# Laying column sums out over the partitions: two TensorE transposes or eight small DMAs

## The chip, the cores and the metric

The kernel runs on one core of a Trainium2 chip. The metric is the device time of one execution in microseconds; the figure that counts is the median of several runs. A profiled execution adds a trace of every instruction on the engines: TensorE (PE, with its weight loads as PEld), VectorE (DVE), ScalarE (ACT), GpSimd (POOL) and SyncE (SP), which in this kernel issues every DMA.

## What is computed

Two layers of a conditioned decoder trunk, for 256 positions of 1024 channels. Each layer is a feed-forward half-step, a token mixer (sparse attention beside a gated MLP), and another feed-forward half-step. Every one of these six sub-layers is entered through an RMS norm with a shift and a scale, and left through a gate, all three computed from one conditioning vector c:

```python
for l in range(DEPTH):
    mod = (jax.nn.silu(c) @ ada_w[l] + ada_b[l]).reshape(B, 3, 3, 1, D)
    n = _modulate(_rmsnorm(h, norm_g[l, 0]), mod[:, 0, 0], mod[:, 0, 1])   # xn * (1 + scale) + shift
    h = h + 0.5 * mod[:, 0, 2] * _swiglu(n, ffn_w_in[l, 0], ffn_w_out[l, 0])
    ...                                    # mixer: mod[:, 1, :], no factor 0.5
    n = _modulate(_rmsnorm(h, norm_g[l, 2]), mod[:, 2, 0], mod[:, 2, 1])
    h = h + 0.5 * mod[:, 2, 2] * _swiglu(n, ffn_w_in[l, 1], ffn_w_out[l, 1])
return _rmsnorm(h, final_g)
```

All is float32. The product of c with `ada_w` is what the change touches: 1024 x 1024 numbers for each of three vectors (m = 0 shift, m = 1 scale, m = 2 gate) of each of six sub-layers (si = 0 to 5).

## The kernel before, in words

The activations lie channel-major: `h` holds 128 partitions x 8 blocks x 256 positions, so channel 128k + p is partition p of block k. A vector over the channels must therefore lie as 128 partitions x 8 columns to be a per-partition scalar of an instruction.

**Weights.** `Stream` (L60 to L163) loads every weight block of 128 x 1024 float32 (`raw`, L116) from SP into one of 26 slots, in one fixed list. A block that goes to TensorE is split in two: `hi` by ScalarE (L134) and `lo` = raw − hi by VectorE (L135). A matmul of the reference becomes three, hi·hi, lo·hi and hi·lo. Blocks are loaded while at most 4 raw blocks (9 in some stretches) are unsplit, and split at most 6 or 7 blocks ahead of their use, so a slot becomes free when TensorE has used its block.

**The products with c.** The blocks of `ada_w` stand in the same list. They never go to TensorE: `ada_item` has VectorE multiply each by the 128 entries of silu(c) that belong to it and add it up in `acc` (128 x 1024, L252 for the first block and L255 for the seven others). What is left is a sum over the 128 partitions. `ada_step` does that in steps; it is called after each output block of a feed-forward sub-layer (L605, L670) and at places in the last product of the mixer (L1208, L1210). In one step, four matmuls with ones (L282) sum the columns of `acc`: quarter t of the 1024 sums lands, replicated, on partitions 32t to 32t + 31 of a PSUM bank, and ScalarE copies the 128 x 256 result into the SBUF tile `adas` (L286, one buffer). In the next step, two transposes on TensorE (L267) turn the sums so that they lie over the partitions; VectorE picks the 8 columns out of the PSUM bank and adds `ada_b` (L271) into the tile `md{si}_{m}`; for the scale it forms (1 + scale)·norm_g (L274), for the gate half of it (L276).

`ada_plan` (L350) says during which sub-layer which vectors are made: 16 of them in this way, four during sub-layer 0, two during 1, four during 2, five during 3, one during 5. All but the two during sub-layer 1 come well ahead of their use. Those two, shift and scale of the second feed-forward sub-layer, (2, 0) and (2, 1), are made inside the last product of the first mixer, by a hook that stands after parts of that product (L1210), some 10 us ahead of the entry that reads them.

**The entry.** `enter` (L418 to L518) begins each later sub-layer. For each of eight channel blocks VectorE adds the gated output of the previous sub-layer to `h` (L439), ScalarE multiplies it by the scale (L441, `uhi`, the hi part) and squares it (L442), and VectorE forms the lo part (L434, `ulo`). The shift enters as two extra columns (L429, L430). TensorE then starts the sub-layer's first product on these (L456) while the norm's factor is still being computed (L463, L400, L414), and the later products run on the normalized `nhi`, `nlo` (L487, L488, L491, L617). The output products of a feed-forward sub-layer and the mixer's last product are `acc_mm` (L563).

**Order.** TensorE, SP and GpSimd run in the order in which the program writes its instructions (`tc.manual_schedule`, L178). The order on VectorE and ScalarE is set by a scheduler at compile time, from its own estimate of when each operand is there, with priorities (`high_priority`) for some.

Of the kernel before, what the change touches and what calls it, by code (L numbers as in the profile page):

```python
# [18 lines left out]
F32 = mybir.dt.float32  # L19
# [147 lines left out]
def trunk(ctx, tc, xT, pk, cst, ada0, win7, ada, win, wou, mixw, mixv, w1, mp, wsT, lngb, bs, out):  # L167
    nc = tc.nc
    V, A, T, G = nc.vector, nc.scalar, nc.tensor, nc.gpsimd

    cp = ctx.enter_context(tc.tile_pool(name="cp", bufs=1))
# [15 lines left out]
    def bank(tag):  # L187
        return ps.tile([128, 512], F32, tag=tag, name=f"{tag}_{uid()}")

    def rbank():  # L190
        cnt["R"] += 1
        return bank(f"R{cnt['R'] % 4}")
# [31 lines left out]
    ident = cst_t[:, C_ID:C_ID + 128]  # L224
# [10 lines left out]
    def norm_g(si):  # L235
        return pk_t[:, 8 + si * 8:16 + si * 8]
# [3 lines left out]
    def ada_b(si):  # L240
        return pk_t[:, 64 + si * 24:88 + si * 24]
# [1 line left out]

    acc = {}
    mods = {}
    ready, summed, clock = [], [], [0]

    def ada_item(si, m, kb):
        def use(raw, slot):
# [10 lines left out]
    def ada_step(now=False):  # L260

        clock[0] += 1
        while summed:
            si, m, sm = summed.pop(0)
            p = rbank()
            for f in range(2):
                T.transpose(p[:, f * 128:(f + 1) * 128], sm[:, f * 128:(f + 1) * 128], ident)  # L267
            with tc.high_priority(PRIO_M):
                t = cp.tile([128, 8], F32, tag=f"md{si}_{m}", name=f"md{si}_{m}")
                v = p[:, 0:256].rearrange("p (f t r) -> p t f r", f=2, r=32)[:, :, :, 0]  # L270
                V.tensor_add(t.rearrange("p (t f) -> p t f", f=2), v,  # L271
                             ada_b(si)[:, m * 8:(m + 1) * 8].rearrange("p (t f) -> p t f", f=2))
                if m == 1:
                    V.scalar_tensor_tensor(t, t, 1.0, norm_g(si), op0=ALU.add, op1=ALU.mult)  # L274
                elif m == 2:
                    V.tensor_scalar(t, t, 0.5, None, op0=ALU.mult)  # L276
            mods[si, m] = t
        while ready and (now or clock[0] >= ready[0][2]):
            si, m, _ = ready.pop(0)
            p = rbank()  # L280
            for t in range(4):
                T.matmul(p[32 * t:32 * t + 32, 0:256], ones[:, 0:32], acc[si, m][:, t * 256:(t + 1) * 256],  # L282
                         start=True, stop=True, tile_position=(0, 32 * t))
            sm = tp.tile([128, 256], F32, tag="adas", name=f"adas{si}_{m}")
            with tc.high_priority(PRIO_M):
                A.activation(sm, p[:, 0:256], AF.Copy)  # L286
            summed.append((si, m, sm))
# [284 lines left out]
    def ffn(si, prev):  # L572
# [21 lines left out]
        if si == 0:  # L594
            with tc.manual_schedule(engines=START_ENGINES):
                x, zb = start()
            for j in range(4):
                evac(j, zb[j])
            accs = [bank(f"A{i}") for i in range(4)]
            for j in range(NS - 1):  # L600
                out_mm(j)
                if j + 4 < NS:
                    evac(j + 4, zb[j + 4])
                st.more()
                ada_step()  # L605
# [56 lines left out]
        for j in range(NS if si == 0 else 4, NF):  # L662
            r = in_mm(j)
            evac(j, r)
            st.more()
            for k in outs_after(si, j):
                out_mm(k)
                if k < NF - TAIL:
                    st.more()
                ada_step()  # L670
# [109 lines left out]
    def mix(si, l, prev):  # L780
# [423 lines left out]
        for kb in range(8 - WGROUP):  # L1204
            acc_mm(accs, [(st.next(), mhi[:, kb], mlo[:, kb])], kb == 0, False)
            st.more()
            if kb >= 2:
                ada_step()  # L1208
# [130 lines left out]
```

## Time and profile before

| quantity | us |
|---|---|
| median of three runs | 1156.9 |
| the three runs | 1155.82, 1156.9, 1160.89 |
| the profiled execution | 1160.77 |
| span of its trace | 1159.0 |
| PE busy | 1137.9 (98%) |
| DVE busy | 879.7 (76%) |
| ACT busy | 599.4 (52%) |

The span is the time from the first to the last instruction in the trace of the profiled execution. Busy time of an engine is the time during which at least one of its instructions ran. The granted TensorE clock is shown beside the trace as a share of full speed; over the span it was 0.987.

### The profile page before, as it was taken

To read this page: it belongs to the slowest core of one execution; us is meant where nothing else is said; L and a number is where in the kernel's file an instruction comes from. 1 tells how busy PE (TensorE), PEld (TensorE's weight loads), DVE (VectorE), ACT (ScalarE), POOL (GpSimd) and SP (SyncE) were. 2 spreads that over 40 slices of the span, in tenths; PEclk is the share of its full clock that TensorE was granted. 3 is DMA by queue.
4 is the path that set the end of the run, shared out by engine and by line. 5 is a ranking of instruction groups with operands and counts; after the bars stand their busy time and mean duration, and the time that the engine had idled before them with its cause. 6 is when DMAs were issued, how large, how long until landed. Compare 5 with 4: busy or idle time off the path is not lost. (4 is left out here: it accounts for less than half of the span.)

```text
span 1159.0 us, 23635 instructions
## 1 busy us (share of the span) xinstructions
PE 1137.9 (98%) x9630; PEld 1096.2 (95%) x9630; DVE 879.7 (76%) x1514; ACT 599.4 (52%) x1020; POOL 9.6 (1%) x13
## 2 busy tenths in 40 slices
PE   8999999989899999999999999999999999999998
PEld 6999999979799999999999999998899899999998
DVE  4998786778977799777579977767886778856543
ACT  3474444655575575444465444356656647544432
POOL 0000000000000000000000000000000000000000
PEclk8999999999999999999999999999999999999998
DMA  9979598438744659987647977974443366766600
GB/s 364 406 255 379 213 356 318 171 114 312 271 161 144 242 195 374 334 296 282 243 159 278 372 264 275 360 284 149 183 147 127 119 224 223 259 215 242 223 26 37
DMA packets 77180, 278.07 MB, mean 240 GB/s; under 512 B 8592, under 2 KB 9104, under 8 KB 77072
## 3 DMA queue, kind: packets, MB, share of 16 engines
q1 hardware_dynamic: 77072, 276.57, 65.1%
q8 instruction: 75, 1.23, 0.4%
q14 instruction: 33, 0.27, 0.1%
HBM read 275.49 MB, written 1.05 MB: 239 GB/s over the span
## 5 line engine op out<-in xcount | busy, mean ns | idle before, releaser
L135 DVE TENSOR_TENSOR lo<-raw,hi 128x1024 fp32r<-128x1024 f32 (+1 forms) x366 | 443.0, 1217 | 127.2 <-ACT hi L134 107.0
L134 ACT ACTIVATE hi<-raw 128x1024 fp32r<-128x1024 f32 (+1 forms) x366 | 381.0, 1052 | 273.3 <-PE R L617 67.0
L563 PE MATMUL A<-s1r,hi 128*128 128x256 f32 x1408 | 255.2, 279 | 0.0
L617 PE MATMUL R<-nhi,hi 128*128 128x256 f32 x1152 | 229.6, 281 | 0.0
L617 PE MATMUL R<-nhi,lo 128*128 128x256 f32 x1152 | 227.1, 279 | 0.0
L617 PE MATMUL R<-nlo,hi 128*128 128x256 f32 x1152 | 226.8, 279 | 0.0
L563 PEld LDWEIGHTS A<-s1r,hi 128*128 128x128 f32 x1408 | 218.9, 189 | 0.2 <-DVE s1r L555 0.2
L563 PE MATMUL A<-s1r,lo 128*128 128x256 f32 x704 | 196.0, 278 | 0.0
L617 PEld LDWEIGHTS R<-nhi,hi 128*128 128x128 f32 x1152 | 174.8, 188 | 5.8 <-issue 5.8
L617 PEld LDWEIGHTS R<-nlo,hi 128*128 128x128 f32 x1152 | 175.3, 189 | 0.0
L617 PEld LDWEIGHTS R<-nhi,lo 128*128 128x128 f32 x1152 | 175.0, 189 | 0.0
L255 DVE SCALAR_TENSOR_TENSOR acc<-raw,sc,acc 128x1024 f32<-128x1024 f32 x112 | 143.4, 1281 | 24.5 <-DMA raw<-in_ada 23.7
L563 PEld LDWEIGHTS A<-s1r,lo 128*128 128x128 f32 x704 | 132.3, 188 | 0.0
L583 ACT ACTIVATE s<-R 128x256 f32<-128x256 f32 x75 | 28.3, 377 | 105.1 <-PE R L617 105.1
L809 PE MATMUL A<-nhi,hi 128*128 128x256 f32 x256 | 74.8, 292 | 0.0
L809 PE MATMUL A<-nhi,lo 128*128 128x256 f32 x256 | 71.8, 280 | 0.0
L809 PE MATMUL A<-nlo,hi 128*128 128x256 f32 x256 | 71.8, 280 | 0.0
L554 ACT ACTIVATE s1r<-s 128x256 fp32r<-128x256 f32 x88 | 36.2, 412 | 47.9 <-DVE s L585 46.7
L585 DVE TENSOR_TENSOR s<-s,R 128x256 f32<-128x256 f32 x75 | 31.2, 416 | 37.1 <-ACT s L583 37.0
L809 PEld LDWEIGHTS A<-nhi,hi 128*128 128x128 f32 x256 | 49.0, 191 | 3.9 <-issue 2.3
L809 PEld LDWEIGHTS A<-nhi,lo 128*128 128x128 f32 x256 | 48.7, 190 | 0.0
L809 PEld LDWEIGHTS A<-nlo,hi 128*128 128x128 f32 x256 | 48.6, 190 | 0.0
(258 smaller groups left out, 1627.5 us busy)
## 6 DMA issues: line engine op xcount, KB each, us to landing
raw<-in_win SPq DMA_DIRECT2D x170, 512.0 KB, 5.7
raw<-in_ada SPq DMA_DIRECT2D x144, 512.0 KB, 5.7
raw<-in_mixw SPq DMA_DIRECT2D x92, 512.0 KB, 3.6
raw<-in_wou SPq DMA_DIRECT2D x88, 512.0 KB, 5.4
raw<-in_mixv SPq DMA_DIRECT2D x8, 536.0 KB, 5.7
w<-in_w SPq DMA_DIRECT2D x8, 512.0 KB, 8.5
raw<-in_win SPq DMA_DIRECT2D x8, 384.0 KB, 9.8
h<-in_xT SPq DMA_DIRECT2D x2, 512.0 KB, 5.5
```

Of the source, the lines that this page charges most:

```text
L134: self.nc.scalar.activation(hi[:, :n], raw[:, :n], AF.Copy)
L135: self.nc.vector.tensor_sub(lo[:, :n], raw[:, :n], hi[:, :n].bitcast(F32))
L255: V.scalar_tensor_tensor(a, raw[:, :D], sc[:, kb:kb + 1], a, op0=ALU.mult, op1=ALU.add)
L554: A.activation(hi_out, src, AF.Copy)
L563: T.matmul(accs[db // 2][:, (db % 2) * S:(db % 2 + 1) * S], w[:, db * 128:(db + 1) * 128], xx, start=(first and i == 0 and p == 0 and db % ...
L583: A.activation(s_, r[:, 0:S], AF.Silu)
L585: V.tensor_mul(g_, s_, r[:, S:2 * S])
L617: T.matmul(r[:, ab * S:(ab + 1) * S], W[:, c0:c0 + 128], xx[:, k], start=(i == 0 and ab == 0), stop=(i == 23), skip_group_check=True)
L809: T.matmul(r[:, b * S:(b + 1) * S], w[:, k], xx[:, k], start=(b == 0 and k == 0 and p == 0), stop=(k == 7 and p == 2), skip_group_check=True)
```

## The change

A vector goes from the sums to its place over the partitions by eight DMAs from SBUF to SBUF, one for each column of 128 channels, in place of the two transposes. Each reads 128 neighbouring numbers of one partition of `adas` and writes one number to each of the 128 partitions of `md`. They are issued from SP, at the step at which the transposes stood. The addition of `ada_b` no longer reads PSUM but `md` in place, and stands one step later, so a vector needs three steps in place of two. One PSUM bank of the ring `R` less is taken for each vector.

```diff
-    ready, summed, clock = [], [], [0]
+    ready, summed, turned, clock = [], [], [], [0]
...
-        while summed:
-            si, m, sm = summed.pop(0)
-            p = rbank()
-            for f in range(2):
-                T.transpose(p[:, f * 128:(f + 1) * 128], sm[:, f * 128:(f + 1) * 128], ident)
+        while turned:
+            si, m, t = turned.pop(0)
             with tc.high_priority(PRIO_M):
-                t = cp.tile([128, 8], F32, tag=f"md{si}_{m}", name=f"md{si}_{m}")
-                v = p[:, 0:256].rearrange("p (f t r) -> p t f r", f=2, r=32)[:, :, :, 0]
-                V.tensor_add(t.rearrange("p (t f) -> p t f", f=2), v,
-                             ada_b(si)[:, m * 8:(m + 1) * 8].rearrange("p (t f) -> p t f", f=2))
+                V.tensor_add(t, t, ada_b(si)[:, m * 8:(m + 1) * 8])
...
             mods[si, m] = t
+        while summed:
+            si, m, sm = summed.pop(0)
+            t = cp.tile([128, 8], F32, tag=f"md{si}_{m}", name=f"md{si}_{m}")
+            for k in range(8):
+                nc.sync.dma_start(t[:, k:k + 1], sm[k // 2 * 32:k // 2 * 32 + 1, k % 2 * 128:k % 2 * 128 + 128])
+            turned.append((si, m, t))
```

The lines of the changed kernel are L276 for the DMAs, L266 for the addition and L268, L270 for what follows it.

**TensorE at the first vector**, the gate of sub-layer 0, between an output product (L563) and the next input product (L617). In the kernel before:

```order
L563 MATMUL A_73_903<-s1r_1514,lo_1423 128x256
L563 MATMUL A_73_903<-s1r_1515,hi_1422 128x256
L267 MATMUL R_112_1665<-cst_t,adas_2_1565 128x128 x2
L617 MATMUL R_113_1671<-nhi_197,hi_1455 128x256 x2
L617 MATMUL R_113_1671<-nhi_197,lo_1456 128x256 x2
```

In the changed kernel:

```order
L563 MATMUL A_73_903<-s1r_1514,lo_1423 128x256
L563 MATMUL A_73_903<-s1r_1515,hi_1422 128x256
L617 MATMUL R_112_1674<-nhi_197,hi_1455 128x256 x2
L617 MATMUL R_112_1674<-nhi_197,lo_1456 128x256 x2
L617 MATMUL R_112_1674<-nlo_198,hi_1455 128x256 x2
```

The pair of transposes is gone and the input product takes the PSUM bank that they had; nothing else moves here.

**SP around the entry to the second feed-forward sub-layer**, whose shift and scale are `md_0_5063` and `md_1_5072` in the changed kernel. In the kernel before:

```order
L116 DMA raw_4985<-in_wou 128x1024
L116 DMA raw_5015<-in_win 128x1024
L116 DMA raw_5142<-in_win 128x1024
L116 DMA raw_5373<-in_wou 128x1024
L116 DMA raw_5379<-in_ada 128x1024
```

In the changed kernel:

```order
L116 DMA raw_5005<-in_wou 128x1024
L116 DMA raw_5035<-in_win 128x1024
L276 DMA md_0_5063<-adas_0_5042 128x1x1 x8
L276 DMA md_1_5072<-adas_1_5049 128x1x1 x8
L116 DMA raw_5172<-in_win 128x1024
L116 DMA raw_5403<-in_wou 128x1024
```

Both groups of eight DMAs stand one behind the other, and every later load behind them.

**ScalarE at the same entry**; `s` are squares, `hi` splits of weight blocks, `uhi` the entry's first operand. In the kernel before:

```order
L134 ACTIVATE hi_5138<-raw_4883 128x1024
L286 ACTIVATE adas_0_5022<-R_400_5017 128x256
L286 ACTIVATE adas_1_5029<-R_401_5024 128x256
L429 ACTIVATE uhi_5144<-md_0_5046 128x8x2
L441 ACTIVATE uhi_5144<-h,md_1_5051 128x256
L442 ACTIVATE s_404_5148<-h 128x256
```

In the changed kernel:

```order
L442 ACTIVATE s_403_5183<-h 128x256
L134 ACTIVATE hi_5399<-raw_4905 128x1024
L134 ACTIVATE hi_5405<-raw_4907 128x1024
L134 ACTIVATE hi_5468<-raw_4909 128x1024
L286 ACTIVATE adas_1_5049<-R_397_5044 128x256
L442 ACTIVATE s_404_5184<-h 128x256
L442 ACTIVATE s_405_5185<-h 128x256
L429 ACTIVATE uhi_5174<-md_0_5063 128x8x2
L199 ACT_TABLE_LOAD
L199 ACTIVATE junk_5225<-s_405_5185 128x1
L134 ACTIVATE hi_5474<-raw_4939 128x1024
L441 ACTIVATE uhi_5174<-h,md_1_5072 128x256 x8
```

The copy of the second vector's sums stood right behind that of the first; now six squares (the first five stand above the rows shown) and three splits stand between them, and all eight products with the scale come after the squares.

**VectorE at the same entry**, from the addition for the shift on. In the kernel before:

```order
L135 TENSOR_TENSOR lo_5139<-raw_4883,hi_5138 128x1024
L271 TENSOR_TENSOR md_0_5046<-R_402_5043,pk_t 128x8
L430 TENSOR_TENSOR ulo_5145<-md_0_5046,uhi_5144 128x8x2
L271 TENSOR_TENSOR md_1_5051<-R_403_5048,pk_t 128x8
L274 SCALAR_TENSOR_TENSOR md_1_5051<-md_1_5051,pk_t 128x8
L439 SCALAR_TENSOR_TENSOR h<-A_396_4877,md_2_2700,h 128x256 x2
```

In the changed kernel:

```order
L439 SCALAR_TENSOR_TENSOR h<-A_395_4900,md_2_2712,h 128x256 x2
L266 TENSOR_TENSOR md_0_5063<-md_0_5063,pk_t 128x8
L135 TENSOR_TENSOR lo_5406<-raw_4907,hi_5405 128x1024
...
L430 TENSOR_TENSOR ulo_5175<-md_0_5063,uhi_5174 128x8x2
L135 TENSOR_TENSOR lo_5469<-raw_4909,hi_5468 128x1024
L449 TENSOR_TENSOR s_398_5178<-s_398_5178,s_399_5179 128x256
L135 TENSOR_TENSOR lo_5475<-raw_4939,hi_5474 128x1024
L266 TENSOR_TENSOR md_1_5072<-md_1_5072,pk_t 128x8
L268 SCALAR_TENSOR_TENSOR md_1_5072<-md_1_5072,pk_t 128x8
L434 SCALAR_TENSOR_TENSOR ulo_5175<-h,md_1_5072,uhi_5174 128x256 x8
```

The two additions stood ahead of all the updates of `h` (L439); now they stand behind all of them, and the second behind three splits as well.

## Rows read from the trace of the kernel before

**Rows 1.** The page: span; busy time of the engines; the TensorE clock and the DMA share in 40 equal slices of the span (tenths); the chain that ended last, by engine.

```profile
span 1159.0 us, 23635 instructions
...
PE 1137.9 (98%) x9630; PEld 1096.2 (95%) x9630; DVE 879.7 (76%) x1514; ACT 599.4 (52%) x1020; POOL 9.6 (1%) x13
...
PEclk8999999999999999999999999999999999999998
DMA  9979598438744659987647977974443366766600
...
PE 28%; DVE 1%; DMA 0%; ACT 0%; issue 0%; ACTq 0%
```

**Rows 2.** The transposes and the addition behind them, each by source line: count, shortest/median/longest in ns, first and last start.

```profile
L267 PE MATMUL R<-cst_t,adas x32: 270/272/328, 126.0 to 1118.8; 128*128 128x128 f32 x32
...
L271 DVE TENSOR_TENSOR md<-R,pk_t x16: 155/164/168, 126.5 to 1119.1; 128x8 f32<-128x8 f32 x16
```

**Rows 3.** Timeline of PE at the first transposes: start in us, duration, instruction (x2: two in a row).

```profile
125.92 0.28 PE L563 MATMUL A<-s1r,hi 128*128 128x256 f32 x1
126.04 0.38 PE L267 MATMUL R<-cst_t,adas 128*128 128x128 f32 x2
126.17 0.48 PE L617 MATMUL R<-nhi,hi 128*128 128x256 f32 x2
126.49 0.40 PE L617 MATMUL R<-nhi,lo 128*128 128x256 f32 x2
```

**Rows 4.** PE alone in stretches between two places at which `ada_step` puts work on PE: window in us, its length, PE busy (instructions that touch the window), granted clock, DMA share, GB/s.

```profile
70.00:117.00 47.00, 47.00 (x417) 1.00 0.89 328
126.50:143.00 16.50, 16.50 (x143) 1.00 0.56 206
144.00:169.50 25.50, 25.50 (x217) 1.00 0.95 353
188.50:207.50 19.00, 19.00 (x163) 1.00 0.78 293
418.00:468.50 50.50, 50.50 (x448) 1.00 0.84 316
478.20:494.80 16.60, 16.60 (x143) 1.00 0.91 309
585.50:593.00 7.50, 7.50 (x66) 1.00 0.34 125
607.00:652.00 45.00, 45.00 (x383) 1.00 0.83 319
687.50:704.00 16.50, 16.50 (x142) 1.00 0.45 154
978.00:1109.00 131.00, 131.00 (x1159) 1.00 0.63 225
1119.20:1142.00 22.80, 22.80 (x196) 1.00 0.01 1
```

**Rows 5.** The entry to the second feed-forward sub-layer, timelines of PE, ACT and DVE (start in us, duration, instruction, and in brackets the idle time before it and what ended it).

```profile
393.94 0.38 PE L267 MATMUL R<-cst_t,adas 128*128 128x128 f32 x2
394.86 0.44 PE L267 MATMUL R<-cst_t,adas 128*128 128x128 f32 x2 [0.53 <-ACT adas L286]
...
404.67 0.40 PE L456 MATMUL R<-uhi,hi 128*128 128x258 f32 x2
...
417.11 0.40 PE L617 MATMUL A<-nhi,hi 128*128 128x256 f32 x2
...
394.42 0.38 ACT L286 ACTIVATE adas<-R 128x256 f32<-128x256 f32 x1 [1.49 <-PE R L267]
...
404.10 1.99 ACT L134 ACTIVATE hi<-raw 128x1024 fp32r<-128x1024 f32 x2
...
408.48 1.28 ACT L199 ACT_TABLE_LOAD   x1
...
404.87 0.88 DVE L439 SCALAR_TENSOR_TENSOR h<-A,md,h 128x256 f32<-128x256 f32 x2
...
408.64 2.36 DVE L135 TENSOR_TENSOR lo<-raw,hi 128x1024 fp32r<-128x1024 f32 x2
```

**Rows 6.** Issues on SP's queue: one load alone at its start and duration, and the page's groups of DMA issues (count, KB each, median us from issue to landing).

```profile
152.54 0.33 SPq L116 DMA_DIRECT2D raw<-in_win  x1
...
raw<-in_win SPq DMA_DIRECT2D x170, 512.0 KB, 5.7
raw<-in_mixw SPq DMA_DIRECT2D x92, 512.0 KB, 3.6
...
out_dram<-o SPq DMA_DIRECT2D x4, 256.0 KB, 2.1
...
pk_t<-in_pk SPq DMA_DIRECT2D x1, 104.0 KB, 2.0
```

**Rows 7.** All engines (PE, PEld, DVE, ACT, POOL busy and counts, then clock, DMA share, GB/s) behind a stretch in which PE idles, at 784.9.

```profile
784.90:788.30 3.40, 1.60 (x11) 1.19 (x11) 3.40 (x9) 3.40 (x9) 0.00 (x0) 1.00 0.56 206
788.30:791.70 3.40, 3.40 (x18) 3.40 (x18) 3.40 (x9) 1.75 (x3) 0.00 (x0) 0.50 0.01 2
```

**Rows 8.** ACT at the two places where a split waits for a load that stands behind a group's place on SP.

```profile
189.22 1.06 ACT L134 ACTIVATE hi<-raw 128x1024 fp32r<-128x1024 f32 x1 [0.73 <-DMA raw<-in_win]
...
758.87 2.27 ACT L134 ACTIVATE hi<-raw 128x1024 fp32r<-128x1024 f32 x2 [0.96 <-DMA raw<-in_win]
```

## The prediction

> **What bounds the kernel now.** The page first [rows 1]: PE is busy for 98% of the span at nearly full clock, and the chain that ended last lies on PE; DVE (76%) and ACT (52%) have slack, and the DMA share falls well below full in most slices. So the time is that of a row of matmuls, and an edit counts if it takes an instruction from that row, changes how far apart its matmuls stand, or makes PE wait. The transposes come next [rows 2]: 32, in 16 pairs. Their 0.27 us is a pipelined duration and no cost: the timeline at the first pair [rows 3] goes from one L563 over the pair and two L617 to the next L617 in 125.92 to 126.49 = 0.57 us. Three ordinary steps are 3 x 0.117 = 0.35, so a pair costs 0.22.
>
> Then the spacing of the matmuls [rows 4]. A window counts every matmul that touches it, about two more than fit. Less two, 70 to 117 gives 47.0 / 415 = 113.3 ns, 418 to 468.5 gives 113.2, 978 to 1109 gives 113.2. But 126.5 to 143 gives 117.0, 144 to 169.5 gives 118.6, 478.2 to 494.8 gives 117.7, 1119.2 to 1142 gives 117.5: at the same granted clock 1.00, PE goes at one of two paces. Contention doesn't explain it: the last stretch is slow with a DMA share of 0.01 and the one of 978 to 1109 is fast with 0.63. What the slow ones share is that a pair of transposes stands right ahead (125.9, 477.8, 1118.7); the fast ones follow the sums (L282) or a sub-layer without vectors. In all I count 17 slow stretches at or after a pair and before the next change of pace, 307 us; the rows show eight of them, the first and the last included. Lastly the entry to the second feed-forward sub-layer [rows 5], where vectors are made at the last moment: there PE goes from L563 to L456 (404.67) without a gap.
>
> **The pairs.** Fourteen pairs outside that entry x 0.22 = 3.1 us, all on the path: **−3.1**. The two at the entry are counted with it. DVE's addition (0.16 us, [rows 2]) only changes its operand.
>
> **The pace.** If all 307 us went at 113.2 in place of 117.6, that is 307 x 3.74% = 11.5 us. By sub-layer: 74 us in the first feed-forward, 2.8; 102 in the second, 3.8; in the third 52 that were slow from its entry on (585.5 to 593 and 607 to 652 have no pair between them) 2.0, and 56 behind further pairs, 2.1; 23 in the last, 0.9. The lower end is 0: the trace shows a pair ahead of the change of pace, not that nothing else would bring it, and the slow pace survived an entry. I take the first and last in full (3.7), since fast stretches stand on their other side, and just over half of the rest (4.2 of 7.9): **−7.9**.
>
> **The entry to the second feed-forward sub-layer.** In its rows [rows 5] both copies of the sums are done at 394.80, the additions follow the transposes at 394.86 at once, and the entry runs pair by pair behind L563. In the changed order the second copy stands on ACT behind six squares and three splits, and this is the one place where a vector has no spare step. Those splits follow the sixth square, which the third update of h releases; the two at 404.10 take 1.99, so three take 3.0. PE is done with L563 about 1 us earlier than now, as the wait of 0.53 and the two pairs are gone. I get three splits from about 401.7 to 404.7 and the copy (0.38) to 405. Then SP issues eight DMAs, each by the nearest row 0.33 us [rows 6], 2.7 us, to 407.7; the last lands 2.0 later by the two smallest transfers of the page (2.0 and 2.1; a load of 512 KB takes 3.6 to 5.7, the upper end), at 409.7. DVE's two short additions and ACT's first product with the scale (0.5) bring L456 to about **411.0**, against 404.67: +6.3, from +5.5 to +8.3. Ahead of these on DVE stand the last updates of h (404.87, 0.9) and three splits of 1.2 us [rows 5], which fit before 409.7, and on ACT a table load of 1.28. The L456 stretch now takes 404.67 to 417.11 = 12.4 us for 96 matmuls, 11.3 at the slow pace: it waits 1.1 for pairs of h, and those waits go, since h is long complete: −1.1. But PE idles some 7 us, and after an idle stretch the clock falls: behind one at 784.9 (busy 1.60 of 3.40) the next 3.40 us have 0.50 and 18 matmuls, 2.1 us of work at the full pace [rows 7], 1.3 lost. I take two such: +2.6. Entry: **+7.8**. Its lower bound is 0, if the scheduler's splits wait for nothing and the copy runs right after the sums; its upper bound 8.3 − 1.1 + 3 x 1.3 = 11.
>
> **SP's queue.** 128 DMAs of 0.33 us are 42 us of issue, off the path. But the last ones of a group wait in the compiled order for the landing of the load issued just ahead, so each group holds back the loads behind it for about 4 us [rows 6]. Splits run well ahead of PE nearly everywhere; at 189 and 759 they wait for a load [rows 8] behind a group's place and little cover is left. From 0 to 2 us each, taken near nothing since PE uses those blocks some 2 us after their split: **+0.5**. DVE's additions stand a step later, 8 us or more, behind the landing.
>
> **What the skill says against it.** Rows 2 and 3 price the transposes at 0.22 us a pair. The Trainium skill, VectorE: DVE Perf Modes, The three transpose paths, warns that a plain DMA copy which transposes by its access pattern is 19 times slower than the DMA's own transpose, 1309 ns for 128 x 128, and its Rules for kernel authors prefer TensorE. Eight of 128 rows by that would be 19 x 1309 / 16 = 1.6 us for a group (an estimate from that page), inside the 4.7 us reckoned above, and the sum stays; 1.6 us for each DMA one behind the other is the rival below. No row here shows such a DMA.
>
> **The sum** is −3.1 − 7.9 + 7.8 + 0.5 = **−2.7** against the profiled execution's 1160.8: 1158.1. That execution lies 3.9 above the median of 1156.9, so on the median's scale it is 1158.1 − 3.9 = 1154.2, rounded to **1154.0**; the rivals are given on that scale too.
>
> **The rivals.**
>
> *The pace returns in full.* For: the slow stretch at 1119 has nothing else near it but the pair. Against: 607 to 652. −3.1 − 11.5 + 7.8 + 0.5 = −6.3: 1150.6.
>
> *The entry is hidden.* The second copy finds its PSUM result and its place earlier than I think, and L456 starts where it does now. For: ACT is idle 1.49 us ahead of 394.42 [rows 5]. Against: the compiled order. −3.1 − 7.9 − 1.1 + 0.5 = −11.6: 1145.3.
>
> *The pace has another cause.* The sums or the loads set it, and only pairs are saved: −3.1 + 7.8 + 0.5 = +5.2: 1162.1, at the border of slower.
>
> *The small DMAs go one behind the other (slower).* A group then takes 8 x 2.0 = 16 us by the smallest transfers [rows 6], in place of 4.7. The entry waits 11.3 longer, and at 189 and 759 the loads behind each group come up to 9 later than cover allows: up to −2.7 + 11.3 + 18 = +27, 1183. It decides from about 3 us more per group on (three places, 8.5 in all). For: each writes 128 partitions one number at a time. Against: the larger loads overlap freely on the same queue. By the skill's 1.6 us each a group would take 12.4, and the time be about 1175.
>
> That the change doesn't do what it says is small here: the transposes are gone from PE's order.
>
> **How the numbers follow.** Forecast 0.42 (1154, its own range 1150 to 1160); full pace 0.24; entry hidden 0.08; other cause 0.13; one behind the other 0.13. A measurement of this kernel tells about 0.5% from no change: 1151.1 and 1162.7. Faster: 0.16 of the full pace, 0.08 and 0.11 of the forecast = 0.35. Slower: 0.13 and 0.05 of the other cause = 0.18. Same: 0.47. The range of 1145 to 1164 leaves out the DMAs one behind the other and a few hundredths on the low side.
>
> **What would show it.** L617 behind 126 at 113 ns in windows like those of rows 4 shows the pace right, 117 shows it wrong; the first L456 of that entry at 411 shows the entry, at 405 the hidden case; issue to landing of the L276 DMAs near 2 us against 10 tells the last rival; clock 0.50 in the stretch behind the entry shows the 2.6. It would be wrong above all if a pair were not what changes the pace, or if SP's queue held more than I see.

## The result, and the profile after

The changed kernel takes 1170.67 us (median of four runs, 1169.82 to 1175.22) against 1156.36 for the kernel before: a ratio of 1.0126, 95% interval 1.0086 to 1.0165, so slower by 14 us (1.3%) where 2 to 3 less were forecast. The profiled execution took 1175.22, 4.6 above its median, and the one of before lay 4.4 above its own (1156.36 is the median of four runs, the 1156.9 on record of three); the two spans, 1173.4 and 1159.0, differ by 14.4, and can be compared piece by piece.

The page of the changed kernel, against [rows 1]:

```profile
span 1173.4 us, 23793 instructions
...
PE 1133.9 (97%) x9598; PEld 1090.9 (93%) x9598; DVE 879.5 (75%) x1514; ACT 600.3 (51%) x1020; POOL 9.7 (1%) x13
...
PEclk8999998999999989999999999989999999999998
...
PE 28%; DVE 1%; DMA 0%; ACT 0%; issue 0%; ACTq 0%
```

PE is busy for 4 us less, though the span is 14 longer: PE waits. The clock row has three new dips, in slices 7, 15 and 27, at about 190, 425 and 780 us; each follows a stretch in which PE idled. The chain's shares look as before: a chain that runs along PE doesn't show waits of 10 us in 1170.

Where it happens is seen by setting the same instruction side by side, the first L456 of each of the five entries, from the two PE timelines, and the length of what lies between:

| PE at | before | after | later by | so this stretch |
|---|---|---|---|---|
| entry 1 (first mixer) | 216.6 | 220.0 | 3.4 | +3.4 |
| entry 2 (second feed-forward) | 404.7 | 417.7 | 13.0 | +9.6 |
| entry 3 (third) | 593.7 | 604.4 | 10.7 | −2.3 |
| entry 4 (second mixer) | 785.0 | 803.7 | 18.7 | +8.0 |
| entry 5 (last) | 964.0 | 981.1 | 17.1 | −1.7 |
| end of the span | 1159.0 | 1173.4 | 14.4 | −2.7 |

There are three losses and, where nothing waits, gains. The first loss is in the last input products ahead of the first mixer; PE, then ACT:

```profile
194.41 0.71 PE L617 MATMUL R<-nhi,hi 128*128 128x256 f32 x2 [3.40 <-ACT hi L134]
195.68 0.79 PE L617 MATMUL R<-nhi,lo 128*128 128x256 f32 x2 [0.55 <-DVE lo L135]
196.27 0.63 PE L617 MATMUL R<-nlo,hi 128*128 128x256 f32 x2
```

```profile
193.31 1.06 ACT L134 ACTIVATE hi<-raw 128x1024 fp32r<-128x1024 f32 x1 [0.97 <-DMA raw<-in_win]
194.57 1.06 ACT L134 ACTIVATE hi<-raw 128x1024 fp32r<-128x1024 f32 x1 [0.21 <-DMA raw<-in_win]
```

PE waits for a split, ACT for a load. Behind the waits the matmuls go in pairs of 0.63 instead of about 0.40, and the granted clock is 0.50, the lower of its two levels (1.2 of 2.4 GHz):

```profile
194.80:198.20 3.40, 2.85 (x14) 2.55 (x14) 3.23 (x3) 2.94 (x3) 0.00 (x0) 0.50 0.57 172
```

The instruction at 188.8 still ran 2.8 us ahead of its time in the kernel before, the one at 201.8 runs 4.3 behind: 7.1 lost. The same picture stands at 774 to 785, from 11.5 behind to 19.0, 7.5 lost; PE there:

```profile
778.15 0.77 PE L617 MATMUL R<-nhi,hi 128*128 128x256 f32 x2 [3.52 <-ACT hi L134]
```

The queue that should have brought the first of those loads:

```profile
151.66 6.14 SPq L276 DMA_DIRECT2D md<-adas  x8
157.91 0.53 SPq L116 DMA_DIRECT2D raw<-in_ada  x1
...
184.82 3.25 SPq L116 DMA_DIRECT2D raw<-in_win  x4
```

The four `in_win` loads for which ACT waits at 193 were issued at 180.41 in the kernel before, now at 184.82. And windows of the DMA share (window, length, PE busy, clock, DMA share, GB/s) show what became of the time, in the changed kernel, then two of them in the kernel before:

```profile
153.00:156.00 3.00, 3.00 (x29) 1.00 0.89 321
156.00:159.00 3.00, 3.00 (x29) 1.00 0.12 6
159.00:162.00 3.00, 3.00 (x29) 1.00 0.94 315
171.00:174.00 3.00, 3.00 (x29) 1.00 0.72 243
```

```profile
156.00:159.00 3.00, 3.00 (x28) 1.00 1.02 414
171.00:174.00 3.00, 3.00 (x29) 1.00 0.93 362
```

While the group holds SP for 6.1 us, what was queued ahead of it lands, and the DMA engines run dry: 0.12 at 156 to 159. In the kernel before they are near full throughout [rows 4: 0.95 from 144 to 169.5], so what isn't moved in the pause has little room later. At 171 the share falls once more: SP issued nothing from 165.33 to 170.95, a wait that the trace puts down to a split (DVE, `lo`) and that the kernel before doesn't have at this size; it follows the pause, though no run shows that it comes of it.

The third loss is the entry of which the prediction knew; SP, ACT, DVE and PE there:

```profile
397.27 17.90 SPq L276 DMA_DIRECT2D md<-adas  x16
...
409.81 0.36 ACT L286 ACTIVATE adas<-R 128x256 f32<-128x256 f32 x1
...
417.13 3.30 ACT L441 ACTIVATE uhi<-h,md 128x256 fp32r<-128x256 f32 x8 [3.78 <-DVE md L268]
...
416.73 0.17 DVE L266 TENSOR_TENSOR md<-md,pk_t 128x8 f32<-128x8 f32 x1 [2.10 <-DMA md<-adas]
```

```profile
417.69 0.80 PE L456 MATMUL R<-uhi,hi 128*128 128x258 f32 x2 [9.76 <-ACT uhi L441]
```

The chain of the forecast stands there link by link: second copy, eight issues, landing, addition, product, PE after 9.8 us of idling. The small DMAs by themselves:

```profile
L276 SPq DMA_DIRECT2D md<-adas x128: 469/599/1607, 118.2 to 1133.2; - x128
...
DMA to landing us min/median/max: 1.9/2.8/7.5
```

And the pace, in windows that answer to [rows 4], in the first, second, third and last feed-forward sub-layer:

```profile
119.00:142.00 23.00, 23.00 (x205) 1.00 0.55 190
512.00:543.00 31.00, 31.00 (x276) 1.00 0.86 321
619.00:663.00 44.00, 44.00 (x375) 1.00 0.84 323
1129.00:1163.00 34.00, 34.00 (x303) 1.00 0.02 2
```

Less the two that touch the edges, 203, 274, 373 and 301 matmuls: 113.3, 113.1, 118.0 and 113.0 ns. Fast where the kernel before was slow in three of them; the third is slow in both, and in the changed kernel it stays slow behind its sums too:

```profile
717.00:741.00 24.00, 24.00 (x206) 1.00 0.83 299
```

(204 matmuls, 117.6 ns.) So there no pair of transposes is needed for the slow pace.

### The profile page after: what moved, and what is told of

Its sections match the earlier page's. It is cut to its first block, busy times and chain, and to the rows that moved or that the text cites. A ratio compares the mean times of both kernels' runs of the same rounds, so it can differ in the third digit from the quotient of the medians.

```text
span 1173.4 us, 23793 instructions
## 1 busy us (share of the span) xinstructions
PE 1133.9 (97%) x9598; PEld 1090.9 (93%) x9598; DVE 879.5 (75%) x1514; ACT 600.3 (51%) x1020; POOL 9.7 (1%) x13
## 5 line engine op out<-in xcount | busy, mean ns | idle before, releaser
L563 PE MATMUL A<-s1r,hi 128*128 128x256 f32 x1408 | 252.0, 277 | 0.0
L617 PE MATMUL R<-nhi,hi 128*128 128x256 f32 x1152 | 229.5, 281 | 6.9 <-ACT hi L134 6.9
L617 PE MATMUL R<-nhi,lo 128*128 128x256 f32 x1152 | 228.1, 280 | 1.0 <-DVE lo L135 1.0
L617 PE MATMUL R<-nlo,hi 128*128 128x256 f32 x1152 | 227.5, 279 | 0.0
L563 PEld LDWEIGHTS A<-s1r,hi 128*128 128x128 f32 x1408 | 217.5, 188 | 0.2 <-DVE s1r L555 0.2
L563 PE MATMUL A<-s1r,lo 128*128 128x256 f32 x704 | 195.0, 277 | 0.0
L617 PEld LDWEIGHTS R<-nhi,hi 128*128 128x128 f32 x1152 | 176.0, 190 | 13.1 <-ACT hi L134 7.3
L617 PEld LDWEIGHTS R<-nhi,lo 128*128 128x128 f32 x1152 | 176.5, 191 | 1.6 <-DVE lo L135 1.6
L617 PEld LDWEIGHTS R<-nlo,hi 128*128 128x128 f32 x1152 | 176.7, 190 | 0.0
L563 PEld LDWEIGHTS A<-s1r,lo 128*128 128x128 f32 x704 | 132.1, 188 | 0.0
```

The source lines that it names most:

```text
L563: T.matmul(accs[db // 2][:, (db % 2) * S:(db % 2 + 1) * S], w[:, db * 128:(db + 1) * 128], xx, start=(first and i == 0 and p == 0 and db % ...
L617: T.matmul(r[:, ab * S:(ab + 1) * S], W[:, c0:c0 + 128], xx[:, k], start=(i == 0 and ab == 0), stop=(i == 23), skip_group_check=True)
```

## The experiments

All were compared with the kernel before. A table of what they gave; "idle" is PE's time beyond 0.113 us a matmul, summed over the steps above 0.15 us in the PE timeline, so waits and matmuls at half clock together, in the 33 us ahead of entry 1, at entry 2 and in the 33 us ahead of entry 4:

| kernel | us | ratio, 95% interval | idle at 194, entry 2, 776 |
|---|---|---|---|
| before | 1156.4 | | 0.6, 0.1, 0.6 |
| after | 1170.7 | 1.0126 [1.0086, 1.0165] | 7.4, 10.0, 7.5 |
| no layout | 1141.0 | 0.9859 [0.9831, 0.9887] | 0.5, 0.1, 0.9 |
| both | 1171.7 | 1.0125 [1.0095, 1.0155] | 6.9, 9 (inside L563), 6.8 |
| hybrid | 1161.4 | 1.0056 [1.0026, 1.0086] | 7.0, 0.1, 7.5 |
| direct | 1178.6 | 1.0182 [1.0150, 1.0213] | 0.1, 0.1, 0.1 |
| shift | 1148.2 | 0.9934 [0.9912, 0.9956] | 0.9, 0.1, 0.6 |
| GpSimd's queue | 1163.3 | 1.0076 [1.0047, 1.0104] | 5.2, 8.9, 3.5 |
| one DMA | 1148.5 | 0.9925 [0.9898, 0.9953] | 0.7, 3.0, 0.5 |
| VectorE | 1146.1 | 0.9920 [0.9889, 0.9951] | 0.8, 0.1, 0.5 |
| before again | 1159.1 | one run | 0.6, 0.1, 0.6 |
| shift by 64 | 1152.5 | 0.9961 [0.9946, 0.9977] | 0.6, 0.1, 0.6 |
| ring of buffers | 1171.2 | 1.0120 [1.0097, 1.0142] | 5.6, 7.8, 8.2 |
| one group | 1161.4 | 1.0043 [1.0023, 1.0063] | 4.2, 0.1, 0.6 |

**No layout (e1).** Neither the transposes nor the DMAs.

```diff
-            p = rbank()
-            for f in range(2):
-                T.transpose(p[:, f * 128:(f + 1) * 128], sm[:, f * 128:(f + 1) * 128], ident)
...
-                V.tensor_add(t.rearrange("p (t f) -> p t f", f=2), v,
-                             ada_b(si)[:, m * 8:(m + 1) * 8].rearrange("p (t f) -> p t f", f=2))
+                V.tensor_add(t, sm[:, 0:8], ada_b(si)[:, m * 8:(m + 1) * 8])
```

> Neither transposes nor DMAs: the addition takes the first 8 columns of the copied sums as they lie (so shift, scale and gate hold wrong numbers), all else as in the kernel before, the order at the entry to the second feed-forward sub-layer too. Theory A (a pair of transposes on TensorE costs its own 0.22 us and leaves the matmuls behind it 117.6 instead of 113.2 ns apart): 11 to 13 us below the kernel before, about 1144. Rival (the pace has another cause, the pairs cost only themselves): 3 to 4 us below, about 1153.

Measured 15.1 less. The matmuls go at 113 ns from the first vector to the last, in the third feed-forward sub-layer as well (a stretch of 44 us that is slow in both the others):

```profile
156.00:159.00 3.00, 3.00 (x29) 1.00 1.02 365
...
119.00:142.00 23.00, 23.00 (x205) 1.00 0.55 197
597.00:639.00 42.00, 42.00 (x372) 1.00 0.83 321
```

(203 in 23.0 and 370 in 42.0 us: 113.3 and 113.5.) So the pace and the pairs together are worth what the prediction put on them, and more, above the 11 to 13 that were expected. It didn't show yet that the pairs make the pace. The first row is the DMA share where the changed kernel has 0.12.

**Both (e2).** The kernel before with its transposes, and the eight DMAs besides.

```diff
             mods[si, m] = t
+            u = cp.tile([128, 8], F32, tag="mdx", name=f"mdx{si}_{m}")
+            for k in range(8):
+                nc.sync.dma_start(u[:, k:k + 1], sm[k // 2 * 32:k // 2 * 32 + 1, k % 2 * 128:k % 2 * 128 + 128])
```

> The kernel before with its transposes, and the eight DMAs of each vector besides, into a tile that nobody reads. Theory B (the groups of DMAs hold SP's queue for 5 to 8 us where the loads are near their limit, and TensorE pays for it at the last input products of the first and fourth sub-layer, 7 us each): 1171 to 1177, stalls at 194 and 776 as in the changed kernel, the pace of before, and some 5 us at the entry to the second feed-forward sub-layer since the second copy of sums waits for the DMAs to have read the first. Rival (the stalls come from the later addition or from another order on ScalarE and VectorE, not from the queue): within 3 us of before, 1154 to 1160.

Measured 15.5 more, with both stalls at nearly their size: the pairs being gone has no part in them, the DMAs make them. At the entry the second pair of transposes waits 8.92 us for the second copy, in the middle of L563:

```profile
396.67 0.38 PE L267 MATMUL R<-cst_t,adas 128*128 128x128 f32 x2
405.97 0.69 PE L267 MATMUL R<-cst_t,adas 128*128 128x128 f32 x2 [8.92 <-ACT adas L289]
```

One thing was not as expected. The pace behind the pairs:

```profile
125.00:141.00 16.00, 16.00 (x143) 1.00 0.65 237
150.50:166.50 16.00, 16.00 (x143) 1.00 0.80 294
518.00:542.00 24.00, 24.00 (x214) 1.00 0.83 311
```

141, 141 and 212 matmuls less the edges: 113.5, 113.5, 113.2. The pairs are all there and the pace behind them is fast. A pair can't be what sets it.

**Hybrid (e3).** The DMAs, but transposes for the two vectors of the second feed-forward sub-layer.

```diff
             si, m, sm = summed.pop(0)
+            if si == 2 and m < 2:
+                p = rbank()
+                for f in range(2):
+                    T.transpose(p[:, f * 128:(f + 1) * 128], sm[:, f * 128:(f + 1) * 128], ident)
...
+                continue
```

> The changed kernel with the transposes put back for the two vectors of the second feed-forward sub-layer alone. Theory B (that entry costs 11 us because the second copy, the eight issues and the landing stand in front of it): 1159 to 1161, L456 right behind L563 again, and the two 7 us stalls stay. Rival (the entry is late because the loads behind are late too): gains 5 us or less, 1165 or more.

Measured 1161.4, at the edge of what theory B gave; its ten runs lie from 1157.5 to 1170.0. The entry's wait is gone, which is worth 8 to 9 us against the changed kernel, the two stalls stay, and so does a loss against the kernel before.

**Direct (e4).** The sums made over the partitions by eight matmuls with the accumulated product as weights.

```diff
+            for k in range(8):
+                T.matmul(p[:, k:k + 1], acc[si, m][:, k * 128:(k + 1) * 128], ones[:, 0:1],
+                         start=(k == 0), stop=(k == 7), skip_group_check=True)
```

> Neither transposes, nor DMAs, nor the copy: the sums are made over the partitions at once, by eight matmuls with 128 columns of the accumulated product as weights and one column of ones as the moving operand; the addition follows in the same step. Theory A, if only the transposes change the pace: 10 to 13 us below the kernel before, 1143 to 1147, with the entry to the second feed-forward sub-layer a little earlier. If any float32 weight load of 128 x 128 changes the pace: about 1154 to 1157.

A miss on both sides, 22 us more. The timeline at the first vector:

```profile
118.73 1.84 PE L282 MATMUL R<-ones,acc 128*128 128x1 f32 x16
120.43 0.48 PE L621 MATMUL R<-nhi,hi 128*128 128x256 f32 x2
```

Eight matmuls stand as sixteen in the trace and take 1.7 us before the next product starts, in place of 0.22 for the pair and some 0.7 for the four sums, and the pace behind them is slow nearly everywhere. No stall: there are no small DMAs.

**Shift (e5).** The kernel before, with one more tile that nobody reads.

```diff
             mods[si, m] = t
+            u = cp.tile([128, 8], F32, tag="mdx", name=f"mdx{si}_{m}")
+            V.memset(u, 0.0)
```

> The kernel before with one more tile of 128 x 8 numbers, set to zero and read by nobody, so that all SBUF tiles behind it lie 32 bytes per partition further on, as they do in the kernel with transposes and unread DMAs; no DMA is added and TensorE's instructions are the same. Theory C (where the tiles lie, or something else that stays the same through a run, decides at which of two paces TensorE goes on behind a pair; the pair itself does not): 113.4 ns behind the pairs, 1144 to 1148. Rival (the pace behind a pair depends on how the DMAs or the waits move the moment of its start): 117.8 as before, 1154 to 1159.

Measured 1148.2, 7 to 8 us less, by a tile without use. Behind the pairs:

```profile
126.50:142.50 16.00, 16.00 (x138) 1.00 0.56 202
152.50:168.00 15.50, 15.50 (x139) 1.00 0.95 358
501.50:525.00 23.50, 23.50 (x210) 1.00 0.92 310
```

117.6 behind the first, then 113.1 and 113.0 where the kernel before has 117 to 118. Theory C holds for all but the first pair and the stretch behind entry 3. By the traces the order of instructions on PE, ACT and DVE is that of the kernel before, but for 16 zeroings of about 0.07 us on DVE, all done by 3.5 us from the start.

**GpSimd's queue (e6).** `nc.sync.dma_start` for the small DMAs becomes `nc.gpsimd.dma_start`.

> The changed kernel with its small DMAs issued from GpSimd's queue in place of SP's. Theory B (the loss is that SP's queue stands still, not what the small DMAs take of the DMA engines): no 7 us stalls at 194 and 776, the entry to the second feed-forward sub-layer still late by 5 to 11, 1148 to 1157. Rival (element by element writes take the DMA engines from the loads): the stalls stay, 1165 or more.

Between the two: 1163.3. The first stall falls from 7.4 to 5.2, the second from 7.5 to 3.5, and what is left has another cause. The loads come in time now: the split that waits for the first of them starts at 187.57, where it stood at 189.22 in the kernel before [rows 8] and at 193.31 in the changed one, and the DMA share at 156 to 159 is 0.71. But the small DMAs land later from here:

```profile
DMA to landing us min/median/max: 1.9/5.0/6.4
```

and on VectorE the addition, which waits until they have landed, stands ahead of a split; that split is late, and PE waits for it (DVE, then PE):

```profile
193.17 0.17 DVE L266 TENSOR_TENSOR md<-md,pk_t 128x8 f32<-128x8 f32 x1 [3.28 <-DMA md<-adas]
```

```profile
194.74 0.50 PE L617 MATMUL R<-nhi,lo 128*128 128x256 f32 x2 [1.78 <-DVE lo L135]
```

At 768.58 VectorE waits 4.36 in the same way, and PE 1.45 for its split. Waits of 0.76 behind a load's split are left at either place. So most of what SP's queue costs is gone in this run, and most of the rest is the addition's place ahead of the splits, with the lower clock behind each wait. The entry is hardly shorter (8.9).

**One DMA (e7).** `for k in range(8)` becomes `for k in range(1)`, with the tile zeroed at the start.

> The changed kernel with the first of the eight DMAs of each vector alone; the other seven columns are zero before ada_b is added, so shift, scale and gate are wrong there. Theory B: a group is one issue of some 0.5 us behind one wait, the stalls shrink to under 1 us each and the entry to 3 to 6 us: 1146 to 1152. Rival (what costs is that any DMA stands in the queue behind a wait for the copied sums): 1160 or more.

1148.5: no stalls, and the entry at 3.0 us. That any DMA stands there is not what costs; the length of the group is. A single one holds SP for about half a microsecond:

```profile
L277 SPq DMA_DIRECT2D md<-adas x16: 470/476/1122, 116.0 to 1102.1; - x16
```

**VectorE (e8).** The four sums read the product in another order of columns, and a mask picks.

```diff
+            av = acc[si, m].rearrange("p (c q i) -> p q c i", q=4, i=32)
             for t in range(4):
-                T.matmul(p[32 * t:32 * t + 32, 0:256], ones[:, 0:32], acc[si, m][:, t * 256:(t + 1) * 256],
+                T.matmul(p[32 * t:32 * t + 32, 0:256], ones[:, 0:32], av[:, t],
...
+                V.tensor_mul(smv, p[:, 0:256].rearrange("p (c i) -> p c i", i=32), m32[0][:, None, :].to_broadcast([128, 8, 32]))
+                V.tensor_reduce(t, smv, axis=AX, op=ALU.add)
+                V.tensor_add(t, t, ada_b(si)[:, m * 8:(m + 1) * 8])
```

> Neither transposes nor DMAs nor the copy: the sums read the accumulated product in another order of columns (blocks of 32 channels), so that each group of 32 partitions holds the channels that belong to it, and VectorE takes the right one of each 32 by a product with a mask and a sum over 32 columns; the addition follows, all in one step. The matmuls on TensorE are the four of the kernel before with a strided moving operand. Theory A or C: the pace stays at 113.4 ns and nothing waits: 1139 to 1144. If the strided operand is read slower or the four sums leave the slow pace: 1150 or more.

1146.1, 2 above the range, and the fastest of those that compute the whole trunk: 10 us below the kernel before, 25 below the changed one, with no stall. One stretch behind entry 3 is slow in it.

**Before again (e9)** and **shift by 64 (e10)**: the kernel before, unchanged, and the unread tile with 16 columns.

> The kernel before, unchanged, for a second trace. Theory C (the pace behind each pair is fixed by what the program is, not by chance of an execution): 117.8 ns behind the same pairs as in the first trace (7 of 8 that come from the fast pace), 113.4 behind the others, and about 1156. Rival (chance): another pattern.

> As the unread tile of 32 bytes per partition, but with 64. If the place of the tiles decides the pace: again another pattern behind the pairs than in the kernel before, of 1144 to 1158 according to it, and the pattern alone explains the time at 0.6 us lost for each 16 us at the slow pace. If the first unread tile was chance: 1156 with the pattern of the kernel before.

The second trace of the kernel before has the same pattern, pair for pair, the odd one out included (fast behind 661.5 in the first, behind 662.2 in the second):

```profile
126.50:143.00 16.50, 16.50 (x145) 1.00 0.58 207
505.70:530.70 25.00, 25.00 (x217) 1.00 0.91 311
...
663.00:679.00 16.00, 16.00 (x145) 1.00 0.96 347
```

(By start times of neighbouring matmuls behind the pairs 117.8, 117.8 and 113.3 ns; the windows end among the sums, whose matmuls count too.) With 64 bytes the pattern is a third one, and the time, 1152.5, lies between. So the pace behind a pair was the same in both executions of a program, and it differs between programs with the same instructions on TensorE. What differed is where the tiles lie, and the short zeroings at the start, more than 100 us ahead of the first pair; that it is the place of the tiles is the likelier of the two, and not shown apart.

**Ring of buffers (e11).** The copied sums go to a ring of eight (`sm = s1()`).

> The changed kernel, but the copied sums go to a ring of eight buffers of that size in place of one buffer; now the second copy stands right behind the first on ScalarE at the entry to the second feed-forward sub-layer. Theory D (the single buffer, read by DMAs, sends the second copy behind the squares and splits, and that is half of the entry's loss): that entry loses 3 to 6 us in place of 12.3, both 7 us stalls stay, 1162 to 1166. Rival (the entry's loss is the queue's alone): 1169 to 1172.

A miss: 1171.2, as the changed kernel. The copy does stand some 12 us further ahead, the 16 DMAs are issued by 407.3, but PE idles for 7.8 at the entry in place of 10.0: DVE takes the addition at 411.55, behind its splits, without a wait for a DMA. The buffer was 2 us of that entry, not half of it, and a gain of that size can't be told in the time.

**One group (e12).** The kernel before, with the DMAs for the vector (1, 0) alone: `if (si, m) != (1, 0):` stands around the transposes.

> The kernel before, with the eight DMAs in place of the transposes for one vector alone, (1, 0), whose group stands on SP some 40 us ahead of the stall at 194. Theory B as the traces now have it (a group empties the DMA engines for some 3 us while they are near full from there to the end of the sub-layer, so what is lost there is missing at 194): a stall of 3 to 6 us at 194 with half clock behind it, none at 776, and 0 to 3 us from another pace either way: 1157 to 1163. Rival (the group that stands right at 191 is what stalls TensorE): no stall, 1153 to 1157.

1161.4, and 4.2 us at 194, the half clock included, with none at 776 and nothing at the entry:

```profile
152.47 6.73 SPq L291 DMA_DIRECT2D md<-adas  x8
```

```profile
195.63 0.50 PE L632 MATMUL R<-nhi,hi 128*128 128x256 f32 x2 [2.32 <-ACT hi L134]
```

A group of 6.7 us at 152 makes PE wait at 193. It is the early group that is paid for at 194, not the one that stands beside it. What is left of the changed kernel's 7.4 would be the other three groups' of that sub-layer, which no run takes singly.

## Why the prediction was wrong

**The step that failed is "SP's queue": +0.5, measured 7.1 + 7.5 = 14.6.** Two things in it were wrong. The price: an issue of a small DMA was put at 0.33 by the row of a large one and took 0.60, and with the waits a group held the queue for 5.0 to 7.8 us in place of about 4. And above all the cover. The prediction asked at each place whether the next blocks were split early enough, and found thin cover at two places. But the blocks' lead is a stock that the loads fill, and the loads had the DMA engines near full from 144 on [rows 4]. A pause there empties the engines (0.12 at 156 to 159) and is not made up until the loads slacken; it is carried along, past 35 us in which no matmul waits, and falls due where the lead is shortest, 40 us later, with the loss by the lower clock on top. The run with one group shows this by itself, the one with both that the DMAs alone do it, the one with one DMA that it is the group's length, and the one with GpSimd's queue that the loads are in time once SP is free.

The slower rival, the small DMAs one behind the other, had the right sign and the two places at 189 and 759 among its three, and not the right cause: they land 2.8 us after issue (median) and overlap, SP is what is slow. From its first issue to its last landing a group took 7.6 us at 152 and 9.2 at 191, against the 4.7 reckoned, so its bound of about 3 us more a group was reached. The rival's words on 1.6 us for each DMA don't follow from the estimate that they use: 19 x 1309 / 16 ns is the price of a whole group of eight, as the prediction itself says where it works it out. By that reading of the Trainium skill, VectorE: DVE Perf Modes, The three transpose paths, a group is still inside the 4.7 us, and the 12.4 and 1175 have no ground. The Trainium skill, DMA: Bandwidth & Descriptors, Rules for kernel authors, says that transfers under 64 KB are mostly overhead, and here that agrees, by the queue: 0.5 KB took SP 0.60 us, 512 KB 0.33 [rows 6].

**The entry: +7.8, measured +11.2.** PE waits 9.9 us longer ahead of L456, less 1.2 for the wait and the pairs that are gone from L563: 8.7 where 6.3 was forecast; behind it 2.5 are lost in place of 2.6 − 1.1 = 1.5. The mechanism was right in each link, the sizes were not: PE was done with L563 at 407.9, the copy ended 2.2 later (predicted 1.3), the eight issues took 5.0 to 415.2 (predicted 2.7), the last landed some 1.5 later (2.0). The hybrid took it away and gained 8 to 9 us.

**The pairs and the pace: −11.0; measured about −9.3** by the stretches of the table less the losses in them: 3.4 − 7.1 = −3.7 ahead of entry 1, −2.3 − 2.5 = −4.8 ahead of entry 3, 8.0 − 7.5 = +0.5, the slow third sub-layer, ahead of entry 4, and −1.3 at the end, where the other 1.4 of the −2.7 come of the closing norm: its matmuls fall to the lower clock later than before. The sum came near for a reason that was half wrong. What the prediction called the effect of a pair is one of two paces that TensorE kept in these traces until something disturbed its row of matmuls. A pair can disturb it; to which pace it then goes on is not the pair's doing, as the shifts and the run with both show, and the third sub-layer of the changed kernel is slow without any. Without pairs the fast pace was kept behind nearly all sums in e1 and e8, and taking them out does bring the gain there; but about half of it, 7 to 8 of 15 us, was to be had with the pairs in place (e5). That the slow pace behind entry 3 might stay was allowed for in the half that was taken. The direction of this term was in part luck: another layout would have given another sum. One reading of the prediction's rows was off: its 118.6 ns for 144 to 169.5 counts the pair at 152.5 in, and the steps between matmuls there are 117.8 apart.

The forecast's small gain was the difference of two large terms, and the queue's was judged at two places only. The DMAs lose 7.1 + 7.5 + 11.2 = 25.8, pairs and pace give back 9.3, the closing norm 1.4 and the two mixers 0.8: +14.4 by the unrounded times.

**What stays open.** What about the layout decides the pace, if it is the layout; two other layouts were tried, and two traces of one. Why the small DMAs land later from GpSimd's queue. How the first stall is shared among the four groups of that sub-layer.

## What to carry to other kernels

That nothing waits beside a pause in a queue doesn't make the pause free if the transfers behind it run near their limit: read the DMA share over the stretch from the pause to the next thin place, and charge the pause there, with the clock that PE loses when it idles. A small DMA held its issuing queue longer than a load of 512 KB, so eight for 4 KB were more than eight times the hold; an engine with slack (VectorE, with a mask and a sum) did the same layout without a wait of TensorE. And before a change of a few microseconds in a row of matmuls is given a cause, run the same kernel with an unread tile: here that alone moved the time by 4 and by 7 to 8 us.

## What the runs showed of the hardware

TensorE went through the same matmuls at about 113.3 or 117.8 ns each at the same granted clock of 1.00, the faster pace for up to 131 us at a time (978 to 1109 in the kernel before, [rows 4]), the same in two executions of a program, and otherwise in a program with 32 or 64 bytes a partition of another tile for each vector (0.9934 and 0.9961 of the time). A matmul with 128 x 128 float32 weights and one moving column (e4; two records each in the trace) took 1.70 / 8 = 0.21 us with its weight load, more than one of 256 columns in the products around it (0.113). An SBUF to SBUF DMA of 128 single numbers held SP for 0.60 us (median), GpSimd for 0.53 (e6). A group of them that held SP for 6.1 us let the DMA share fall to 0.12, and TensorE waited about 40 us later.
